# Hybrid decoder layer on one core: the buffers in which the gate groups' block sums lie

## The chip, the cores and the metric

One Trainium2 chip, one of its cores. The metric is the time of one execution on the device in microseconds, as the median of several runs. The profile is taken from one execution by the hardware profiler; it lists every instruction on the core's engines: TensorE (PE, with its weight loads PEld), VectorE (DVE), ScalarE (ACT), GpSimd (POOL) and the queues that start transfers (SyncE, SP, and POOL).

## The reference

One decoder layer over 512 tokens of width 2048, in float32. Three groups of heads (8 gated linear attention heads "GLA", 4 forgetting attention heads "FoX", 4 cross-attention heads on a memory of 256 tokens) read the same normalised input through one projection. Their outputs are normalised per head and multiplied by gates, which are projections of the same input; the result goes through an output projection and, with a residual, through a squared-ReLU MLP.

```python
xn = rms_norm(h, attn_norm_g)
proj = xn @ w_in
(gq, gk, gv, gg, ga, fq, fk, fv, fg, ff, mq, mg) = split(proj)
gla_o = gla_chunked(gq, gk, gv, log_sigmoid(ga @ gla_a_w2 + gla_a_b) / 16)
fox_o = forgetting_attention(rms_norm(fq), rms_norm(fk), fv, log_sigmoid(ff + fox_f_b))
mem_o = softmax(rms_norm(mq) @ mk.T * HEAD_DIM ** -0.5) @ mv
o = rms_norm(concat[gla_o, fox_o, mem_o], out_norm_g)
gate = concat[silu(gg), sigmoid(fg), sigmoid(mg)]
h = h + (o * gate) @ w_out
u = relu(rms_norm(h, mlp_norm_g) @ w_up)
h = h + (u * u) @ w_down
```

In FoX a query block of 128 rows attends to the causal prefix: row block t has t+1 key blocks, with a mask inside the last one.

## The kernel before, in words

Float32 products are made from three matmuls on split operands: each operand is written as a high part (a cast, on ACT) and the rest (a subtraction, on DVE), and `mm3` (L155 to L159) issues high-high, high-low and low-high. The large products (part of the input projection, the output projection and the MLP) use a Strassen-like scheme with seven products, whose left operands are the blocks a11, a12, a22 of a matrix and four sums of its blocks: s1 = a21 + a22, s2 = s1 - a11, s4 = a12 - s2, s3 = a11 - a21. `block_sums` (L239 to L257) makes them, in the order s1, s2, s4, s3, and yields each with its index; its additions are all recorded at L244.

The middle part of the kernel runs two things beside each other. `projections()` yields after every step of a plain projection: the memory's keys and values, then the column groups fv, mq, and then the gates gg0, gg1, fg and mg. One step (a k) of a gate group is 12 matmuls of 128x512 at L157 to L159. `steps()` is the attention: GLA, then the FoX softmax, then the memory heads' softmax. A small loop (L1137) traces one projection step and then, when its turn has come, one attention step. The order of TensorE in this part is fixed afterwards to the order in which the code was traced (L1145). On the other engines the framework orders the instructions by priority (the place in the code, moved ahead by `tc.high_priority`) and by when their inputs and buffers are there; what it settles is fixed when the program is built.

The softmax goes through banks of one PSUM tile (class `Bank`, L918). A FoX bank holds 4 // n heads of row block t, n = t + 1 key blocks; the row blocks run from t = 3 down to t = 0, which makes 4, 4, 2 and 1 banks. A bank has three parts:

- `one`: the logits `lg` on TensorE (L878, L881); the mask added on DVE into a tile `ls` from tag "ta" (L889 for one head, L895 for several); the row maximum `nmx` (L892 or L896); the exponentials `p` on ACT (L938).
- `two`: the transposes `pT` of `p` on TensorE (L946) and their copy by ACT (L948).
- `three`: the product `av` with the values on TensorE (L957), 1/sum on DVE (L963) and the scaling into `o` (L965).

In one turn of `softmax_heads` (L967) come `three` of the bank before last, `two` of the last and `one` of the next, all at a priority moved ahead by 1000. Memory banks have the same parts, but `rowmax` (L911) reads the logits where they are and uses no `ls`.

When a gate group's projection is done, `gate(n, ps)` (L1054) is traced. It takes four PSUM banks `ps`, multiplies them by the tokens' scale into `zs` (L1062, at the `urgent` priority, which frees the banks), and makes for each of the four an activation tile `e` (named ee_...): |z|, exp, log and a subtraction (`log_sigmoid`, L582 to L585), exp (L1066), for gg0 and gg1 a product with z (L1068), and then the product into `ot`, a part of `o` (L1069). When all four are done, `block_sums` takes the blocks of `ot`, and each block or sum goes either to DRAM through POOL's queue (L1082) or, where the operand's home is ready (`high` is filled by `place()`, after the memory softmax), into the split operands (L1079, L1080).

A tile that is asked for by `tmp(name, tag)` (L175) is one of a few buffers that the tag owns. In this part of the kernel

```python
TAGS = dict(ta=3, tb=2, tc=3, td=2, bT=1, eb=1, rbx=1)     # L478
```

each of 128 x 512 f32. For the groups gg0, gg1 and fg the activations take "bT", "eb", "td", "td" in this order (L1064); s2 and s4 take "td", and s1 and s3 take "ta" (L1072). For the last group, mg, the activations take "tc", s1 and s3 "tb". "bT" and "eb" were also used by GLA, which is over when the first gate comes; "ta" is also used by GLA and by FoX's `ls`. gate(0), of group gg0, is traced in the middle of the FoX banks: directly ahead of the turn with the second bank of row block 1 (heads 2 and 3). gate(1) comes at the end of the memory banks.

Of the kernel before, what the change touches and what calls it, by code (L numbers as in the profile page):

```python
# [47 lines left out]
def hybrid_layer(  # L48
# [126 lines left out]
    def tmp(name, tag, n=512, dt=F32):  # L175
        return tp.tile([128, n], dt, tag=tag, name=name, bufs=TAGS[tag])
# [62 lines left out]
    def block_sums(a11, a12, a21, a22, temp, eng=V):  # L239

        s1, s2, s4, s3 = (temp(v) for v in ("s1", "s2", "s4", "s3"))

        def add(dst, a, b, op):
            eng.tensor_tensor(dst, a, b, op=op)  # L244

        yield A11, a11
        add(s1, a21, a22, ALU.add)
        yield S1, s1
        add(s2, s1, a11, ALU.subtract)
        yield S2, s2  # L250
        add(s4, a12, s2, ALU.subtract)
        yield S4, s4
        add(s3, a11, a21, ALU.subtract)
        yield S3, s3
        yield A12, a12
        yield A22, a22
# [4 lines left out]
    def urgent():  # L261
        return tc.high_priority(offset=2 * AHEAD)
# [264 lines left out]
    def lower(i, cs):  # L527

        if i != S2:
            return low[i][0][:, cs]  # L530
        if cs.start < CUT:
            assert cs.stop <= CUT
            return low[i][0][:, cs]
        return low[i][1][:, cs.start - CUT : cs.stop - CUT]
# [19 lines left out]
    def halves(ap):  # L554
        return ap.rearrange("p (j t) -> p j t", j=2)
# [23 lines left out]
    def log_sigmoid(dst, z, e):  # L579

        n = z.shape[0]
        A.activation(e, z, AF.Abs)  # L582
        A.activation(e, e, AF.Exp, scale=-1.0)
        A.activation(e, e, AF.Ln, bias=one_c[:n, :])
        V.scalar_tensor_tensor(dst, z, 0.0, e, op0=ALU.min, op1=ALU.subtract)  # L585
# [468 lines left out]
    def gate(n, ps):  # L1054
        group, silu = gates[n]
        ot, last = heads_of[n], n == 3

        zs = [sc[:, :4, :].rearrange("p h t -> p (h t)"), sc[:, 4:, :].rearrange("p h t -> p (h t)")]
        zs += [ql.rearrange("p h s i -> p (h s i)") for ql in qls]
        with urgent():  # L1060
            for z, bank in zip(zs, ps):
                V.tensor_mul(z, bank, late["rbg"])  # L1062
        for i, z in enumerate(zs):
            e = tmp(f"ee_{group}_{i}", "tc" if last else ("bT", "eb", "td", "td")[i])  # L1064
            log_sigmoid(e, z, e)
            A.activation(e, e, AF.Exp)  # L1066
            if silu:
                V.tensor_mul(e, e, z)  # L1068
            V.tensor_mul(ot[:, i, :], ot[:, i, :], e)  # L1069

        def temp(v):
            return halves(tmp(f"{v}_{group}", "td" if v in ("s2", "s4") else "tb" if last else "ta"))  # L1072

        cs = slice(n * 512, n * 512 + 512)
        for i, src in block_sums(ot[:, :2, :256], ot[:, 2:, :256], ot[:, :2, 256:], ot[:, 2:, 256:], temp):
            early = i in (A11, S1) or i == S2 and not last
            if early and high:
                hi, lo = halves(high[i][:, cs]), halves(lower(i, cs))
                A.copy(hi, src)  # L1079
                V.tensor_sub(lo, src, hi.bitcast(F32))  # L1080
            else:
                nc.gpsimd.dma_start(halves(out_op[i][:, cs]), src)  # L1082
                if early:
                    waiting.append((i, cs))
# [70 lines left out]
    for q in range(3):  # L1155
        _, _, made = w_first.split(1, q)
# [328 lines left out]
```

## Time and profile before

| | us |
|---|---|
| median of 3 runs | 2157.89 (2155.65 to 2158.06) |
| the profiled execution, its time | 2158.14 |
| the profiled execution, its span | 2156.4 |

Busy time of the engines in the profiled span: PE 98%, PEld 81%, DVE 75%, ACT 53%, POOL 9%. The mean granted TensorE clock is 0.992.

The stages that matter here, from the start of the span: the FoX banks run from about 490 to 570 us, the memory banks from about 573 to 615 us; the four gates start at 536.4, 624.8, 669.3 and 712.8 us; the output projection's first products run from about 714 us.

How to read the views. The page lists for every group of instructions the line, engine and operation, `out<-in` by the program's names with buffer numbers left out (so all four sums of a group gg0 or gg1 are `s_gg`, and the activations `ee_gg`), shapes and count. The view of waits says which engine and line waited for which, with the total, the number of times and the longest. The chain that ended last is followed back from the last instruction: each step leads to what released it. The timeline gives start, length, engine, line, and in brackets the engine's idle time ahead of the instruction and what ended it. The table by stretch gives, for each stretch of time, its length, the busy time of PE, PEld, DVE, ACT and POOL with the number of instructions, the granted TensorE clock (1.00 is full), the share of the DMA engines and GB/s.

### The profile page before, as it was taken

How to read it: one execution, taken by the hardware profiler on the slowest of the kernel's cores; microseconds unless marked ns; L12 is line 12 of the kernel's file. 1: busy time of each engine (PE TensorE's matmuls, PEld its weight loads, DVE VectorE, ACT ScalarE, POOL GpSimd, SP SyncE). 2: the span in 40 equal slices, each digit the busy share in tenths (PEclk: the TensorE clock that was granted, in tenths of full speed). 3: DMA queues.
4: the chain of work that ended last, by engine and by line, in shares of the span. 5: the costliest groups of instructions: out<-in, count | busy, mean ns of one | idle time of the engine just before them, and what ended most of it. 6: DMA issues, size and time to landing. Idle time of an engine off the chain costs nothing.

```text
span 2156.4 us, 25544 instructions
## 1 busy us (share of the span) xinstructions
PE 2109.7 (98%) x9746; PEld 1736.5 (81%) x9746; DVE 1615.8 (75%) x1723; ACT 1132.9 (53%) x1603; POOL 192.7 (9%) x236
## 2 busy tenths in 40 slices
PE   8999999999899899999999999999999999999999
PEld 7877778887688788788888888888788788888787
DVE  7779896773564889967767767778868767777875
ACT  7554373444563565655555555556546546555543
POOL 0252200000000022100000000000100000000000
PEclk9999999999899999999999999999999999999999
DMA  8544242221234575353453353356577678668653
GB/s 273 167 138 146 79 154 79 69 69 49 74 101 138 217 264 203 117 190 113 146 195 120 134 195 127 128 194 221 189 205 230 170 188 262 172 178 269 177 166 130
DMA packets 78755, 347.09 MB, mean 161 GB/s; under 512 B 9305, under 2 KB 13401, under 8 KB 57130
## 3 DMA queue, kind: packets, MB, share of 16 engines
q1 hardware_dynamic: 58778, 274.95, 36.9%
q0 software_dynamic: 19856, 70.53, 12.4%
q8 instruction: 76, 1.25, 0.2%
q14 instruction: 45, 0.37, 0.1%
HBM read 271.52 MB, written 73.92 MB: 160 GB/s over the span
## 4 chain that ended last, share of the span: by engine, by line
PE 78%; DVE 10%; DMA 6%; issue 3%; ACT 2%; POOL 1%; SPq 0%; ACTq 0%; DVEq 0%; POOLq 0%
PE acc_up L157 9%; PE acc_up L159 9%; PE acc_up L158 9%; PE acc_dn L158 7%; PE acc_dn L159 7%; PE acc_dn L157 7%; PE acc_out L158 2%; PE acc_out L157 2%; DVE hl_hl_in L334 2%; PE acc_out L159 2%; DMA left1l<-op 2%; PE gg L157 1%; DVE raw_dn L296 1%; DVE hl_dn L334 1%; PE gg L159 1%
## 5 line engine op out<-in xcount | busy, mean ns | idle before, releaser
L334 DVE TENSOR_TENSOR hl_up<-raw_up,hl_up 128x1024 fp32r<-128x1024 f32 x224 | 271.5, 1222 | 143.6 <-ACT hl_up L334 143.6
L334 ACT CAST hl_up<-raw_up 128x1024 fp32r<-128x1024 f32 x224 | 235.2, 1052 | 255.3 <-PE acc_up L159 196.2
L334 DVE TENSOR_TENSOR hl_dn<-raw_dn,hl_dn 128x1024 fp32r<-128x1024 f32 x224 | 270.5, 1221 | 104.5 <-ACT hl_dn L334 103.9
L334 ACT CAST hl_dn<-raw_dn 128x1024 fp32r<-128x1024 f32 x224 | 234.6, 1053 | 210.9 <-PE acc_dn L159 165.7
L296 DVE TENSOR_TENSOR raw_dn<-raw_dn,raw_dn 128x2048 f32<-128x2048 f32 x64 | 146.0, 2285 | 15.6 <-DMA raw_dn<-in_w_down_dram 15.4
L296 DVE TENSOR_TENSOR raw_up<-raw_up,raw_up 128x2048 f32<-128x2048 f32 x64 | 145.1, 2267 | 2.0 <-DMA raw_up<-in_w_up_dram 1.9
L1400 POOL DMA_DIRECT2D hd<-m x48 | 41.6, 866 | 514.5 <-ACT m L1399 514.5
L334 ACT CAST hl_out<-raw_out 128x1024 fp32r<-128x1024 f32 x56 | 58.6, 1051 | 54.0 <-PE acc_out L159 41.2
L334 DVE TENSOR_TENSOR hl_out<-raw_out,hl_out 128x1024 fp32r<-128x1024 f32 x56 | 68.9, 1251 | 15.3 <-ACT hl_out L334 15.2
L1399 ACT COPY m<-acc_dn 128x512 f32<-128x512 f32 x96 | 54.6, 586 | 32.2 <-PE acc_dn L159 32.2
L1292 POOL DMA_DIRECT2D op<-u x32 | 17.1, 534 | 488.3 <-ACT u L1301 481.2
L158 PE MATMUL acc_dn<-hl_dn,left 128*128 128x512 f32 x128 | 50.3, 393 | 5.5 <-DVE hl_dn L334 5.5
L158 PE MATMUL acc_in<-hl_hl_in,sh 128*128 128x512 f32 x128 | 50.4, 394 | 5.3 <-DVE hl_hl_in L334 5.3
L157 PE MATMUL gg<-ahi_x,hl_gg 128*128 128x512 f32 x128 | 54.5, 426 | 0.0
L157 PE MATMUL acc_up<-hl_up,left 128*128 128x512 f32 x128 | 51.2, 400 | 3.1 <-ACT z L1355 3.1
L334 DVE TENSOR_TENSOR hl_hl_in<-spare,hl_hl_in 128x1024 fp32r<-128x1024 f32 x31 | 43.8, 1424 | 11.0 <-ACT hl_hl_in L334 11.0
L158 PE MATMUL acc_dn<-hl_dn,left0h 128*128 128x512 f32 x128 | 50.3, 393 | 1.3 <-DVE hl_dn L334 1.3
L157 PE MATMUL acc_in<-hl_hl_in,sh 128*128 128x512 f32 x128 | 50.0, 390 | 1.0 <-ACT o L451 1.0
L159 PE MATMUL gg<-ahi_x,hl_gg 128*128 128x512 f32 x128 | 51.0, 398 | 0.0
L158 PE MATMUL gg<-alo_x,hl_gg 128*128 128x512 f32 x128 | 50.9, 398 | 0.0
L158 PE MATMUL acc_up<-hl_up,left 128*128 128x512 f32 x128 | 50.8, 397 | 0.0
L334 ACT CAST hl_hl_in<-spare 128x1024 fp32r<-128x1024 f32 x31 | 32.4, 1048 | 35.0 <-DVE spare L430 12.7
(545 smaller groups left out, 6284.1 us busy)
## 6 DMA issues: line engine op xcount, KB each, us to landing
raw_up<-in_w_up_dram SPq DMA_DIRECT2D x64, 1024.0 KB, 4.8
raw_dn<-in_w_down_dram SPq DMA_DIRECT2D x64, 1024.0 KB, 6.4
hd<-m POOLq DMA_DIRECT2D x48, 512.0 KB, 5.4
raw_out<-in_w_out_dram SPq DMA_DIRECT2D x16, 1024.0 KB, 5.5
op<-u POOLq DMA_DIRECT2D x32, 512.0 KB, 3.1
op<-s POOLq DMA_DIRECT2D x24, 512.0 KB, 2.9
spare<-in_w_pair_dram SPq DMA_DIRECT2D x16, 512.0 KB, 4.2
raw_in<-in_w_pair_dram SPq DMA_DIRECT2D x16, 512.0 KB, 3.7
```

Of the source, the lines that this page charges most:

```text
L157: T.matmul(ps, lhsT=ah, rhs=bh, start=start, stop=False, skip_group_check=on)
L158: T.matmul(ps, lhsT=ah, rhs=bl, start=False, stop=False, skip_group_check=on)
L159: T.matmul(ps, lhsT=al, rhs=bh, start=False, stop=stop, skip_group_check=on)
L296: V.tensor_sub(dst, a, b)
L334: made = A.copy(hi, part), V.tensor_sub(lo, part, hi.bitcast(F32))
L1292: nc.gpsimd.dma_start(down_op[c][i][:, half * 1024 : half * 1024 + 1024], tile)
L1399: A.copy(st[:, t * 512 : t * 512 + 512], acc[t])
L1400: nc.gpsimd.dma_start(dst, st.rearrange("p (t n) -> p t n", t=2), accum_op=ALU.add)
```

## The change

The tags of two of the four sums of the gate groups change. For gg0, gg1 and fg, s1 is drawn from "bT", where the group's own first activation lay, and s3 from "eb", where the second one lay. s2 and s4 stay in "td", and the last group stays as it was. The numbers of buffers stay.

```diff
         def temp(v):
-            return halves(tmp(f"{v}_{group}", "td" if v in ("s2", "s4") else "tb" if last else "ta"))
+            tags = dict(s1="tb" if last else "bT", s2="td", s3="tb" if last else "eb", s4="td")
+            return halves(tmp(f"{v}_{group}", tags[v]))
```

## The prediction

> **What bounds the kernel now.** I read the page first, then TensorE's waits, then the chain that ended last, and last DVE's order around the one place the chain leaves TensorE for long.
>
> ```profile
> span 2156.4 us, 25544 instructions
> PE 2109.7 (98%) x9746; PEld 1736.5 (81%) x9746; DVE 1615.8 (75%) x1723; ACT 1132.9 (53%) x1603; POOL 192.7 (9%) x236
> ```
>
> TensorE is busy 2109.7 of 2156.4 us. Work taken from DVE or ACT is worth nothing unless TensorE waits for it, so the question is which of its 46.7 idle us the change touches. The view of waits, kept to TensorE, longest total first (total, times, longest):
>
> ```profile
> PE pT_f L946 <- ACT p_f L938: 9.9, 1, 9.9
> PE acc_dn L158 <- DVE hl_dn L334: 6.7, 7, 1.8
> ```
>
> The longest single wait is 9.9 us: the transposes of a FoX softmax bank (`two`, L946) wait for the exponentials `p` (L938). The chain in order of time (start, length, what) shows why they were late:
>
> ```profile
> 539.13 0.44 PE pT_f L946 x4
> ...
> 540.94 0.31 PE lg_f L881
> 541.25 0.43 PE gg L157
> ...
> 544.20 0.91 PE av_f L957 x8
> 545.13 0.42 DVE o L965
> 545.55 0.60 DVE o L1069
> ...
> 551.25 1.29 DVE s_gg L244 x2
> 552.54 0.60 DVE ls L895
> 553.14 0.60 DVE s_gg L244
> 553.74 0.61 DVE nmx_f L896
> 554.37 0.61 ACT p_f L938 x2
> 555.02 1.18 PE pT_f L946 x4
> 556.20 0.43 PE lg_f L878 x2
> ...
> 560.41 0.72 PE gg L157
> ...
> 565.69 0.89 PE av_f L957 x8
> ```
>
> The logits of this bank (row block 1, heads 2 and 3) end at 541.25, where the next matmuls begin. The mask tile `ls` that reads them begins at 552.5: over 11 us late. Between lies gate group gg0's arithmetic on DVE (L1069 and its neighbours) and then two block sums, L244 twice; only then comes `ls`, and then two more sums.
>
> DVE was not full at the time. Its order around the logits, and the mask tile of the bank before (535.55):
>
> ```profile
> 535.55 0.69 DVE L895 TENSOR_TENSOR ls<-lg_f,cmask 128x512 f32<-128x512 f32 x1 [1.72 <-PE lg_f L881]
> 541.03 0.16 DVE L963 RECIPROCAL rc_f<-sm_f 128x2 f32<-128x2 f32 x1
> 542.02 0.69 DVE L585 SCALAR_TENSOR_TENSOR ee_gg<-scores,ee_gg 128x512 f32<-128x512 f32 x1 [0.84 <-ACT ee_gg L584]
> 543.59 0.69 DVE L1068 TENSOR_TENSOR ee_gg<-ee_gg,scores 128x512 f32<-128x512 f32 x1 [0.87 <-ACT ee_gg L1066]
> 551.25 1.29 DVE L244 TENSOR_TENSOR s_gg<-o 128x512 f32<-128x512 f32 x2
> ```
>
> DVE stood idle 0.84 and 0.87 us, in brackets, with the logits of 541.25 already there for the second gap. So `ls` was held by the order, not by load. L963 and L965 (545.13) belong to the same softmax turn as `ls`, written after the gate in the code, and go ahead of the gate's rest; their higher priority works. `ls` alone does not profit.
>
> The two sums just ahead of it read only `o`: by the formulas these are s1 (a21+a22) and s3 (a11-a21). In the code s3 is the last of the four; here it stands second. s1 and s3 are exactly the two tiles that draw from tag "ta", from which `ls` draws as well, and gate(0) is written ahead of this `ls`. My reading: buffers of a tag are handed out in the order of the code, so `ls` could not be placed until s1 and s3 had been, and these need the whole gate.
>
> **The change, part by part.** It adds and removes no instruction. All tiles keep 128x512 f32, and each tag its number of buffers, so no address moves.
>
> (1) s1 and s3 of gg0 leave "ta". `ls` then needs only a buffer last used by an earlier `ls`. The stall's 9.9 us go, but for what is late next. For that: in the bank before, `ls` ran at 535.55 and the second exponential at
>
> ```profile
> 538.33 0.49 ACT L938 ACTIVATE p_f<-ls,nmx_f 128x256 f32<-128x256 f32 x1
> ```
>
> which ends at 538.82, 3.3 us after `ls` began. From 541.25 this gives 544.55; one gate step of 0.69 more ahead on DVE and one of 0.6 to 0.7 on ACT give up to 545.9. TensorE reaches the transposes at 545.1 (544.20 plus 0.91). Residue 0 to 0.8 us. The next bank (four heads of 128 columns) has the same cover, 12 gg matmuls and av (541.25 to 545.1, 3.9 us), for a chain that I put at the same 3.3 to 4.6 us: 0 to 0.7. I take 0.7 of the 1.5 in all, the middle: against it the bank before met its transposes without a wait (TensorE's waits hold one entry for pT_f), for it there was less gate work then.
>
> (2) The slow clock behind the stall goes. Length, then busy time of each engine, granted clock, DMA:
>
> ```profile
> 545.00:555.00 10.00, 0.09 (x1) 0.00 (x0) 9.70 (x16) 4.37 (x10) 3.88 (x6) 0.67 0.27 99
> 547.00:548.50 1.50, 0.00 (x0) 0.00 (x0) 1.50 (x4) 1.13 (x2) 0.25 (x1) 0.94 0.00 0
> 555.00:565.70 10.70, 10.68 (x30) 8.01 (x31) 1.72 (x4) 2.69 (x11) 0.54 (x1) 0.51 0.23 79
> 565.70:575.00 9.30, 9.30 (x52) 8.06 (x52) 5.16 (x9) 5.08 (x9) 0.00 (x0) 1.00 0.18 57
> 660.00:714.00 54.00, 54.00 (x240) 44.74 (x239) 27.88 (x33) 23.56 (x32) 2.57 (x4) 1.00 0.41 138
> ```
>
> From the mean of 0.67 the clock halves 3.4 us into the idle stretch (0.94 in 547.0 to 548.5 says the same), and TensorE runs 555.0 to 565.7 at 0.51. Term by term: transposes 1.18 against 0.44 (539.13), 0.74 saved; 12 gg matmuls, 560.41 to 565.69, 5.28 against 541.25 to 544.20, 2.95, so 2.33 saved; logits of four heads, 556.20 to 560.41, 4.21. No warm row has their shape. Half is 2.1; from above, two heads of 256 columns took 539.57 (539.13 and 0.44) to 541.25, 1.68, so four of 128 take at most 3.4. Saved 0.8 to 2.1; I take 1.65, nearer the half, because the clock halves most of it. Sum 4.7, ends 3.9 and 5.2.
>
> [...]
>
> (3) The gate's rest is put off by what goes ahead of it: `ls` 0.69 and its maximum (553.74) 0.61 on DVE, two exponentials on ACT (554.37). Nothing of TensorE waits for it: the products that free the gg banks (L1062) are urgent and keep their place; the finished sums go to DRAM through POOL and are fetched much later:
>
> ```profile
> 555.23 0.54 POOL L1082 DMA_DIRECT2D oo<-s_gg  x1 [0.36 <-DVE s_gg L244]
> 608.86 0.55 POOL L548 DMA_DIRECT2D left0l<-oo  x1 [53.09 <-PE lg_m L909]
> 644.06 1.15 POOL L1082 DMA_DIRECT2D oo<-s_gg  x2 [2.04 <-DVE s_gg L244]
> L582 ACT ACTIVATE ee_gg<-scores x4: 614/625/636, 537.2 to 626.8; 128x512 f32<-128x512 f32 x4
> L582 ACT ACTIVATE ee_fg<-scores x2: 617/625/633, 670.0 to 671.2; 128x512 f32<-128x512 f32 x2
> ```
>
> The price of lost cover: DVE did 9.7 us in the idle stretch, and in the 20 us behind it only 1.72 and 5.16. With the stall and the slow clock gone these 16.6 us of DVE work meet 30 - 14 = 16 us of TensorE; the overhang is gate work, which falls behind the last FoX bank, and if it did not give way it would cost its 0.6 us.
>
> (4) The new neighbours. s1 now follows group gg0's own first activation in "bT", s3 the second in "eb", one buffer each. Their last readers (L1069) are on DVE itself and stand ahead of the sums anyway: 0. The next group's first activation now waits until s1 has been read out. gg0's last sum is sent by 555.8, the next use is at 626.8; gg1's s3 is sent by 645.2, fg's second activation is at 671.2: 0, with margins of 71 and 26 us less the transfer. The last group's tiles are as before. For gg1 and fg no `ls` follows, so nothing is gained there.
>
> (5) Behind 565.7 TensorE works at full clock without a gap until the output projection (54.00 of 54.00 in 660 to 714), so an earlier TensorE hands its gain down whole.
>
> Sum: 9.9 + 4.7 - 0.7 = 13.9 us; ends 9.9 + 3.9 - 1.5 = 12.3 and 9.9 + 5.2 = 15.1. The profiled execution took 2158.14 us (span 2156.4 and 1.7 around it), 0.25 above the median 2157.89. 2158.14 - 13.9 = 2144.2, at the median 2144. With the spread of the runs before (2155.65 to 2158.06) and an order elsewhere shifted a little, this case spans 2141 to 2147.
>
> **The rivals.**
>
> Crowding: the bank's chain gets in among gate steps that wait on ACT and DVE in turn, and a stall of 3.4 us or more stays. From there the clock falls as well (0.94 in 547.0 to 548.5), so the 4.7 us stay too: gain at most 6.5 us, 2151.5, at 6 us of stall 2154. For it: both of DVE's gaps at 542 and 543.6 were ended by ACT's gate steps, so ACT is the fuller of the two, and the exponentials run there. Against: such a stall needs five or six gate steps of 0.6 to 0.7 us ahead of a chain that has priority over them, and the bank before had no wait.
>
> Nothing happens: `ls` is late because the gate stands ahead of it in the code, whatever the buffers. 2158. Against it: L963 and L965 pass the gate, and s3 stands out of its order just ahead of `ls`.
>
> Slower: the shared single buffers make ACT wait at 671.2 for the transfer of gg1's s3 (POOL, 644.06 and 1.15 us). ACT also makes the weights' high parts, so TensorE would stop behind it. It decides against the change only if the transfer ends over 18 us behind 671.2 (13.9 gained and 4.3 for 0.2%), that is over 40 us later than now: 2162 or more. Its entry on POOL waited for nothing but the sum (2.04 us, DVE).
>
> **How the numbers follow.** The first case has 0.80, crowding 0.09, nothing 0.07, slower 0.04. Within 0.2% (4.3 us) counts as no change, about what a measurement of this kernel can tell. Faster holds the first case and nearly all crowding, 0.88; same 0.08; slower 0.04. The range 2140 to 2151 holds the first case with a margin for a shifted order, and reaches to the good end of crowding; left out are the last two cases (0.11) and the bad end of crowding.
>
> **What would show it.** Right: TensorE's waits have no pT_f row near 9.9; `ls` of the second two-head bank begins between 541 and 543, ahead of all four sums; granted clock 1.00 from 545 to 555; the fg and mg groups stand about 14 us earlier, and the gaps at the output projection are as they were. Wrong: `ls` still behind L244; a wait of pT_f or av_f of some us at 545 to 553 with the clock at 0.5 behind it; or new waits of ACT at L582 for a DMA.

## The result, and the profile after

The changed kernel took 2146.25 us (median of 4 runs, 2144.88 to 2148.26) against 2157.97 us (4 runs, 2155.65 to 2160.42): a ratio of 0.9945 with a 95% interval of 0.993 to 0.996, some 12 us less. The profiled execution took 2146.72 us. First its page:

```profile
span 2145.0 us, 25543 instructions
PE 2104.4 (98%) x9746; PEld 1732.6 (81%) x9746; DVE 1615.4 (75%) x1723; ACT 1134.3 (53%) x1603; POOL 191.7 (9%) x236
```

Every engine of that line has the same number of instructions as before. Of TensorE's waits, the pT_f row, which was the longest single wait with 9.9 us, has become short:

```profile
PE pT_f L946 <- ACT p_f L938: 0.5, 1, 0.5
```

DVE in order of time shows the mask tile of the second two-head bank at its new place:

```profile
544.33 0.69 DVE L895 TENSOR_TENSOR ls<-lg_f,cmask 128x512 f32<-128x512 f32 x1 [0.18 <-PE lg_f L881]
...
556.48 0.66 DVE L244 TENSOR_TENSOR s_gg<-o 128x512 f32<-128x512 f32 x1
```

`ls` now starts when its logits end (the bracket: 0.18 us of idle time, ended by the logits). The first of the four sums comes 12 us later, where before two of them stood ahead of it. The chain through the same stretch:

```profile
547.24 0.89 PE av_f L957 x8
548.13 0.44 PE pT_f L946 x4
548.57 0.22 PE lg_f L878 x2
...
551.06 0.43 PE gg L157
...
554.00 0.02 issue
554.02 1.05 ACT hl_gg L149
555.07 1.18 ACT p_f L938 x6
...
556.62 0.23 PE gg L157
```

The transposes at 548.13 follow `av` without a gap and take 0.44 us. A smaller wait has come up one bank later, at 554 to 556.6: the chain leaves TensorE for ACT, a cast of weights and then exponentials. ACT there, from the end of the bank's first exponential to the start of its second:

```profile
553.32 0.19 ACT L938 ACTIVATION_READ_ACCUMULATOR p_f<-ls,nmx_f 128x1 f32 x1
554.02 1.05 ACT L149 CAST hl_gg<-raw_gg 128x1024 fp32r<-128x1024 f32 x1 [0.51 <-PE gg L159]
554.98 0.40 ACT L938 ACTIVATE p_f<-ls,nmx_f 128x128 f32<-128x128 f32 x1
```

ACT stands idle for 0.51 us until TensorE is done with the cast's buffer, and only behind the cast come the other exponentials. The stretches that had clocks of 0.67 and 0.51:

```profile
545.00:555.00 10.00, 9.99 (x55) 8.11 (x53) 7.50 (x16) 8.92 (x20) 0.77 (x1) 1.00 0.17 52
555.00:565.70 10.70, 10.06 (x48) 8.21 (x49) 10.55 (x17) 6.04 (x15) 3.63 (x6) 1.00 0.63 221
```

Full clock in both, and TensorE busy 9.99 of 10.00 where it was busy 0.09.

The whole time moves by a few us from run to run, so I compare kernels by the interval from the first FoX logits to the first matmul of group fg on TensorE; it holds everything that the change touches in group gg0. These are rows of before and then of after; the first start is the number behind the three durations:

```profile
L878 PE MATMUL lg_f<-fkT,fqT x32: 379/486/596, 489.8 to 559.6; 128*128 128x512 f32 x8, 128*128 128x384 f32 x8, 128*128 128x256 f32 x8, 128*128 128x128 f32 x8
L157 PE MATMUL fg<-ahi_x,hl_fg x64: 389/389/487, 625.7 to 670.4; 128*128 128x512 f32 x64
```

```profile
L878 PE MATMUL lg_f<-fkT,fqT x32: 275/484/595, 492.9 to 550.5; 128*128 128x512 f32 x8, 128*128 128x384 f32 x8, 128*128 128x256 f32 x8, 128*128 128x128 f32 x8
L157 PE MATMUL fg<-ahi_x,hl_fg x64: 389/389/487, 615.7 to 660.4; 128*128 128x512 f32 x64
```

With the trace's full digits that is 135.82 us before and 122.80 after: 13.0 us less. Cut at the first memory logits, 83.43 became 70.00 (13.4 less) and the rest 52.40 became 52.80 (0.4 more). That 0.4 begins at the first memory bank. DVE in the changed kernel, whose logits of that bank end at 563.89:

```profile
564.15 1.23 DVE L150 TENSOR_TENSOR hl_gg<-raw_gg,hl_gg 128x1024 fp32r<-128x1024 f32 x1
565.29 0.68 DVE L912 TENSOR_REDUCE nmx_m<-lg_m 128x2 f32<-128x512 f32 x1
```

The row maximum (L912) begins 1.4 us behind the end of its logits, directly behind the subtraction that makes the rest of the next weights (L150); in the kernel before it began 0.27 us behind them.

The span fell by only 11.4 us. The difference lies outside: the first FoX logits came at 492.87 instead of 489.83, 3.0 us later, although no engine's order differs ahead of them, and the stretch behind fg's first matmul was 1.5 us shorter (1529.3 against 1530.8).

### The profile page after: what moved, and what is told of

Read it like the earlier page. It is cut to its first block, busy times and chain, and to the rows that moved or that the text cites. A ratio compares the mean times of both kernels' runs of the same rounds, so it can differ in the third digit from the quotient of the medians.

```text
span 2145.0 us, 25543 instructions
## 1 busy us (share of the span) xinstructions
PE 2104.4 (98%) x9746; PEld 1732.6 (81%) x9746; DVE 1615.4 (75%) x1723; ACT 1134.3 (53%) x1603; POOL 191.7 (9%) x236
## 4 chain that ended last, share of the span: by engine, by line
PE 80%; DVE 9%; DMA 6%; issue 3%; ACT 2%; POOL 1%; SPq 0%; ACTq 0%; DVEq 0%; POOLq 0%
PE acc_up L157 9%; PE acc_up L158 9%; PE acc_up L159 9%; PE acc_dn L158 7%; PE acc_dn L159 7%; PE acc_dn L157 7%; PE acc_out L158 2%; PE acc_out L157 2%; PE acc_out L159 2%; DMA left1l<-op 2%; DVE hl_dn L334 2%; PE gg L157 1%; PE gg L159 1%; PE gg L158 1%; DVE raw_dn L296 1%
## 5 line engine op out<-in xcount | busy, mean ns | idle before, releaser
L157 PE MATMUL acc_up<-hl_up,left 128*128 128x512 f32 x128 | 50.6, 396 | 3.1 <-ACT z L1356 3.1
L157 PE MATMUL gg<-ahi_x,hl_gg 128*128 128x512 f32 x128 | 53.6, 418 | 0.0
L334 DVE TENSOR_TENSOR hl_hl_in<-spare,hl_hl_in 128x1024 fp32r<-128x1024 f32 x31 | 44.0, 1430 | 11.5 <-ACT hl_hl_in L334 11.4
L157 PE MATMUL acc_up<-hl_up,left0h 128*128 128x512 f32 x128 | 50.5, 394 | 0.0
L157 PE MATMUL acc_up<-hl_up,left5h 128*128 128x512 f32 x128 | 50.5, 394 | 0.0
L157 PE MATMUL acc_up<-hl_up,left1h 128*128 128x512 f32 x128 | 50.5, 394 | 0.0
```

What stands on the lines that cost most here:

```text
L157: T.matmul(ps, lhsT=ah, rhs=bh, start=start, stop=False, skip_group_check=on)
L334: made = A.copy(hi, part), V.tensor_sub(lo, part, hi.bitcast(F32))
```

## The experiments

### One sum moved at a time

Theory: within a tag, buffers are handed out in the order of the code, so the mask tile comes behind every older tile of its tag. Rival: the tag is one buffer short. First s1 alone:

```diff
-"td" if v in ("s2", "s4") else "tb" if last else "ta"
+dict(s1="tb" if last else "bT", s2="td", s3="tb" if last else "ta", s4="td")[v]
```

> Only s1 moves to "bT"; s3 stays in "ta". I judge by the interval from the first FoX logits to the first matmul of group fg on TensorE: 135.83 us in the kernel before, 122.80 us in the changed one. Theory (a tag's buffers are handed out in the order of the code, so the mask tile `ls` comes behind every older tile of its tag): `ls` still waits for s3, but s3 needs only the first two activations, whose last product L1069 ended at 547.95 in the profile of before; `ls` at about 548.6 instead of 552.5, the transposes' wait 9.9 -> 5 to 6 us, the clock still falls behind it, interval about 131.5 us, time about 4 us below before. Rival (the tag is one buffer short for the two sums and `ls`): one sum less frees a buffer, the whole gain, interval about 123 us, time 12 to 13 us below before.

Interval 132.40 us, 3.4 less than before; time 2154.0 us, ratio 0.9984 (0.9972 to 0.9995). The wait, and the chain that leads to it:

```profile
PE pT_f L946 <- ACT p_f L938: 7.2, 1, 7.2
```

```profile
549.56 0.60 DVE ee_gg L1068
550.16 0.60 DVE s_gg L244
550.77 0.60 DVE ls L895
551.37 0.60 DVE o L1069
```

Now one sum, not two, stands ahead of `ls`, and `ls` follows it at once. It can only be s3: a product L1069 of a later activation comes behind it (551.37), and s1 needs them all. A part of the gain, as the theory says. The wait is 7.2 and not 5 to 6 us because two more gate steps of 0.6 us (the L1068 at 549.56 and one ahead of it) stood between the second L1069 and s3; I had put s3 directly behind it.

Then s3 alone:

```diff
-"td" if v in ("s2", "s4") else "tb" if last else "ta"
+dict(s1="tb" if last else "ta", s2="td", s3="tb" if last else "eb", s4="td")[v]
```

> Only s3 moves to "eb"; s1 stays in "ta". Theory (order of the code within a tag): s1 needs all four activations, so `ls` stays behind the whole gate; it gains at most the 0.6 us of s3's addition ahead of it. Wait of the transposes 9.3 to 9.9 us, interval from the first FoX logits to fg's first matmul 135.2 to 135.8 us, time within 0.1% of before. Rival (one buffer short): the whole gain, interval about 123 us, time 12 to 13 us below before.

Interval 135.15 us, 0.7 less than before; time 2157.55 us, ratio 0.9998 (0.9988 to 1.0008).

```profile
PE pT_f L946 <- ACT p_f L938: 9.8, 1, 9.8
```

```profile
551.66 0.60 DVE s_gg L244
...
553.50 0.70 DVE o L1069
...
554.23 0.69 DVE s_gg L244
554.92 0.60 DVE ls L895
```

s3 has moved off to 551.66, free of `ls`, and `ls` again follows directly the one sum that still shares its tag, s1, which stands behind the last L1069. With one sum out of the tag in either case, a missing buffer would have shown the same gain twice. It is which tile shares, not how many.

### The tags as before, the sums traced later

```diff
-        cs = slice(n * 512, n * 512 + 512)
-        for i, src in block_sums(...):
-            ...
+        def sums():
+            cs = slice(n * 512, n * 512 + 512)
+            for i, src in block_sums(...):
+                ...
+        if n:
+            sums()
+        else:
+            held.append(sums)
...
+                if held and group == "gg1" and k == 3:
+                    held.pop()()
```

> All tags as in the kernel before (s1 and s3 in "ta"); only the four sums of gg0 and their transfers are traced later, after the third k of group gg1, behind the last FoX bank. Theory (order of the code within a tag): no `ls` is younger than s1 and s3, so the wait of 9.9 us is gone without any change of buffers; interval from the first FoX logits to fg's first matmul 122 to 124 us, time 11 to 14 us below before. Rival (the place itself counts, the softmax needs the buffers of "ta" for itself, or the sums profit from lying in "bT" and "eb"): s1 and s3 lie in "ta" as before, interval 130 us or more.

(k is counted from 0: the condition `k == 3` is the fourth step of gg1.)

Interval 122.33 us; time 2144.7 us (4 runs), ratio 0.9936 (0.9919 to 0.9952). DVE:

```profile
542.97 0.69 DVE L895 TENSOR_TENSOR ls<-lg_f,cmask 128x512 f32<-128x512 f32 x1 [0.18 <-PE lg_f L881]
...
558.22 1.29 DVE L244 TENSOR_TENSOR s_gg<-o 128x512 f32<-128x512 f32 x2
```

With every buffer where it was before, the wait is gone. So the gain is not in where s1 and s3 lie, but in no `ls` being younger than a sum of its tag. The 0.47 us by which this interval is shorter than the changed kernel's lie in the memory banks (52.35 against 52.80). There the row maximum goes ahead of the subtraction for the weights:

```profile
562.57 0.69 DVE L912 TENSOR_REDUCE nmx_m<-lg_m 128x2 f32<-128x512 f32 x1
563.17 1.22 DVE L150 TENSOR_TENSOR hl_gg<-raw_gg,hl_gg 128x1024 fp32r<-128x1024 f32 x1
```

### The wait filled

```diff
             pT = abank(f"pT_{self.name}")
+            if self.name == "f1_2":
+                for _ in range(42):
+                    T.matmul(pT, lhsT=xh[0][:, :128], rhs=xh[0], start=True, stop=True)
```

> The kernel before, with 42 matmuls of 128x512 whose result is overwritten at once, put on TensorE just ahead of the transposes that wait 9.9 us. They fill about 9.6 us of that wait; nothing comes earlier, only the clock does not fall. This measures the second term by itself. My sum put it at 4.7 us (3.9 to 5.2): granted clock 1.00 from 545 to 566, interval from the first FoX logits to fg's first matmul about 131.1 us instead of 135.83. [...]

Interval 131.49 us, 4.3 less than before; time 2156.87 us, ratio 0.9994 (0.9985 to 1.0004). The whole time thus fell by only 1.0 us (between 3.2 less and 0.9 more), and a gain of 4.3 lies outside that interval: part of it at least is lost again elsewhere. In this profile the stretch behind fg's first matmul is 2.5 us longer than in the kernel before (1533.3 against 1530.8); over the eight profiles it lies between 1525.4 and 1534.0, and what takes the gain back is open. The experiment measures the slow clock in its own stretch, not in the whole time. The stretches and the chain (lines behind the addition are three higher: L949 is L946, L960 is L957, L968 is L965):

```profile
545.00:555.00 10.00, 10.00 (x49) 8.25 (x47) 9.66 (x17) 4.37 (x9) 3.38 (x6) 1.00 0.22 78
555.00:565.70 10.70, 10.26 (x53) 8.05 (x52) 3.84 (x7) 4.85 (x15) 1.04 (x2) 1.00 0.31 102
```

```profile
545.75 0.42 DVE o L968
...
556.14 0.44 PE pT_f L949 x2
...
562.02 0.89 PE av_f L960 x8
```

The clock stays at 1.00 in both stretches, and from the transposes to the next `av` it takes 562.02 - 556.14 = 5.88 us, where it took 10.67. So the slow clock cost 4.8 us. The interval shows 4.3 because the transposes came 10.4 us after the break in the chain (545.75 to 556.14) instead of 9.9.

### The changed kernel again, and the softmax ahead of the weights

```diff
     def softmax_heads(parts):
...
-            with tc.high_priority(offset=1000):
+            with tc.high_priority(offset=4000):
```

> The changed kernel once more, beside the next one on the same chip. If the 3.0 us by which its first FoX logits came later than in the profile of before are chance (no instruction ahead of them changed its order), they come between 489.8 and 492.9 us here too, at a place of their own; the interval from them to fg's first matmul, 122.80 us, repeats within 0.3 us. If the change costs them, they come at 492.5 or later again. Time 11 to 14 us below before.

> The changed kernel, with the softmax turns moved ahead by 4000 instead of 1000 in priority, so that the four exponentials of the last FoX bank stand ahead of ACT's cast of gg1's next weights (L149) instead of around it. In the changed kernel the cast stands between the first and the second exponential, and the transposes behind them end 1.5 us later than a full clock and no wait would give. Theory (that cast is the rest of the stall): 1.2 to 1.5 us less, interval from the first FoX logits to fg's first matmul 121.3 to 121.6 us. Rival (the cast then comes late itself, and TensorE waits for weights, or later turns lose as much): 122.5 us or more. In the whole time neither can be told from the changed kernel (within 0.2% of it).

The changed kernel again: first FoX logits at 489.88 us, interval 122.91; time 2145.28 us (5 runs), ratio 0.9944 (0.9931 to 0.9957). The 3.0 us at the start were chance: over all eight profiles, with the same order ahead of that point, it lies between 489.83 and 492.87.

The softmax first: interval 121.04 us, 1.8 less than the changed kernel; time 2144.31 us (6 runs), ratio 0.9934 (0.9921 to 0.9946), not told apart from the changed kernel's. Its chain at the last FoX bank, and ACT there:

```profile
551.21 0.89 PE av_f L957 x8
552.10 0.44 PE pT_f L946 x4
552.54 0.23 PE gg L157
```

```profile
551.70 0.19 ACT L938 ACTIVATION_READ_ACCUMULATOR p_f<-ls,nmx_f 128x1 f32 x1
551.79 1.04 ACT L149 CAST hl_gg<-raw_gg 128x1024 fp32r<-128x1024 f32 x1
```

The cast follows the last exponential, and from the end of the 12 gg matmuls it takes 1.33 us (551.21 to 552.54) to the next ones; in the changed kernel it took 2.62 (554.00 to 556.62). So that cast, standing between the exponentials, cost 1.3 us. Up to the first memory logits this kernel is 1.3 us shorter (68.69 against 70.00), and behind them 0.45 (52.35 against 52.80). The weights, cast later, held up nothing. Together that is 1.8 us, more than the 1.2 to 1.5 expected: the memory banks' turns were moved ahead as well. The 0.45 are the first memory bank's transposes. The loads of TensorE for them wait in the changed kernel (both profiles of it), and in neither the kernel before nor this one, where L912 goes ahead of L150 again:

```profile
PEld pT_m L946 <- ACT p_m L938: 0.6, 2, 0.4
```

## Why the prediction was right, point by point

The cause. That s1 and s3 held up `ls` by sharing a tag was read in the prediction from the order alone: a high-priority step that does not pass, the last sum of the code standing second, DVE idle beside a ready input. The changed kernel and three experiments show it: s1 moved alone leaves `ls` directly behind s3, s3 moved alone leaves it directly behind s1, and with the tags untouched but the sums younger than `ls` the wait vanishes.

Term 1, the stall of 9.9 us: gone at its own bank, with no residue (transposes at 548.13 directly behind `av`).

Term 2, the slow clock: forecast 4.7 (3.9 to 5.2), 4.8 in the changed kernel (548.13 to 554.00 is 5.87 us, against 10.67) and with the wait filled. The logits of four heads, for which there was no row at full clock, take 2.49 us there (548.57 to 551.06), against 4.21: 1.72 saved, 1.65 taken. Where the clock came back is in the last section.

The residue: forecast 0.7 for both banks with ends 0 and 1.5; 0 at the first and 1.3 at the second. This is the mis-sized term: 0 to 0.7 was forecast for the second bank. That 1.3 lies inside the ends for both together is luck, since the first bank had none. I counted gate steps on ACT in front of the chain and left out the cast of the next weights (L149), which has still higher priority (3000 against 1000), waits for TensorE to free its buffer and stands between the exponentials of one bank.

Term 3, the gate's rest, which "falls behind the last FoX bank" and, if it did not give way, "would cost its 0.6 us": 0.4 was lost in the memory banks, but not shown to be by this. DVE is busy 10.55 of 10.70 us just ahead, yet what stands directly ahead of the late row maximum is L150, the weights again. In the run with the sums traced later the last two sums also stand just ahead of that bank (560.03 and 560.74, its logits end at 562.53); there L912 goes ahead of L150, and nothing is lost. That the size is near the forecast is luck.

Sum of what is shown: 9.9 + 4.8 - 1.3 = 13.4 us up to the memory logits, measured 13.4; less 0.4 behind them, 13.0. Forecast 13.9; the 0.9 that is missing is 0.6 more of residue (1.3 for 0.7) and 0.4 in the memory banks, less 0.1 by which the slow clock cost more. The groups fg and mg, forecast about 14 us earlier, stand 10.0 earlier from the start of the span, and 13.0 counted from the first FoX logits. The span gave 11.4 because of 3.0 us at the start, shown to be chance, and 1.5 us the other way behind fg, where the changed kernel's two profiles differ by 3.9 us.

The rivals. Crowding happened on a small scale, one bank later than I had placed it, by the weights' cast and not by gate steps alone; TensorE's wait was 0.5 us and the clock stayed at 1.00. That ACT would be the fuller engine held for the changed kernel (8.92 us against 7.50 on DVE from 545 to 555), not for the stall before (4.37 against 9.70). The 3.4 us at which the prediction lets the clock fall is the value of one stall and no limit: in other waits it fell sooner, after 2.1 and 2.2 us (last section). "Nothing happens" is excluded by `ls` at 544.33, ahead of all four sums. The shared single buffers cost nothing: no wait of ACT at L582 is ended by a transfer.

## What to carry to other kernels

When a step of high priority runs late although its input is there and its engine has gaps, look at what stands directly ahead of it in the engine's order and which buffers the two share: a tag shared by an urgent stream and a slow one lets the slow one's older request hold up the urgent one, even with a buffer free (here the last reader of the `ls` before was done at 538.82, and the next `ls` came at 552.54). The cure is a tag of its own, one whose last use is the slow stream's own, or tracing the slow request later; the last two were run here. When you price a stall on TensorE, add the half clock behind it, here 4.8 us behind a wait of 9.9, and when you price what is left, list everything on the feeding engine with a higher priority than the step you freed.

## What the runs showed of the hardware

After 9.9 us of idle time the granted clock stayed at about half (0.50) for 10.4 us of work (555.0 to 565.4). With s1 alone moved, a wait of 7.2 us was followed by half clock (0.50) from 553.2 to about 562. With the wait filled by matmuls it did not fall there at all (1.00 from 545.0 to 565.7). Two rows of the kernel with s1 alone moved:

```profile
559.00:562.00 3.00, 3.00 (x8) 2.31 (x8) 1.23 (x3) 1.65 (x8) 0.00 (x0) 0.52 0.15 51
562.00:565.00 3.00, 3.00 (x21) 2.66 (x20) 0.96 (x2) 1.57 (x2) 0.00 (x0) 1.00 0.00 0
```

The clock is back in the second. In both cases the return came while the gg matmuls ran back to back (from 560.41 in the kernel before, 558.6 in this one), and not during the transposes and the small logits ahead of them. In the kernel before, TensorE was busy for 1.98, 2.00 and 2.00 us of the three stretches of 2 us from 555.0 to 561.0, which hold that earlier work, and the clock stood at 0.50 in each. No run varied the work, so what brought the clock back is open.

The clock of the traces also shows when it fell. TensorE had been idle for 3.2 us in the kernel before (545.09 to 548.32) and for about 2.1 us with s1 alone moved (546.1 to about 548.2; the mean from 548.0 to 551.0 is 0.53). In the kernel before, a later wait of 3.1 us (907.96 to 911.09) had lasted 2.2 us when the clock fell at 910.14. The slow stretches took 17.07 us (548.32 to 565.39), about 13.7 us (548.2 to 561.9) and 6.8 us (910.14 to 916.96). These are three cases, and they show no single length of a wait behind which the clock falls.
